# Hybrid decoder step on one core: order of the Mamba-2 scans, their decay rows and the state readouts in the mixer

## Chip, core and metric

The kernel runs on one core of a Trainium2 chip. A core has five engines that run beside each other, each through its own queue in order: TensorE (PE, matmuls and transposes; its weight loads are shown apart as PEld), VectorE (DVE), ScalarE (ACT), GpSimd (POOL) and SyncE (SP), which here only issues DMAs. The time is the device time of one execution in microseconds (us).

## What is computed

One step of a decoder trunk of depth 1 over 520 tokens: 512 of a new prompt and 8 samples that each carry on a sequence of their own. FFN1, a mixer and FFN2 follow each other, all float32. The mixer has two heads beside each other, and the change lies in the second one:

```python
proj = h @ w_in
u_pool, z, xbc, dt_raw = split(proj)
pool_out = pool_mix(u_pool)                       # causal means over 2, 4, 8, 16 tokens, then a matmul per group
xs, Bm, Cm = split(silu(causal_conv(xbc)))        # 1024 + 2*128 + 2*128 features
dt = softplus(dt_raw + dt_bias)
Acs = cumsum(dt * A)                              # within a chunk of 128 tokens, for each of 16 heads
y_diag = einsum(scores, exp(seg), dt, xc)         # inside the chunk
states = einsum(Bc, exp(Acs[-1] - Acs) * dt, xc)  # what the chunk adds to the state
...
y_off = einsum(Cc, h_prev, exp(Acs))              # what the state gives to the chunk
y = (y_diag + y_off + d_skip * xs) * silu(z)
y = rms_norm_per_group(y) * ssd_norm
out = concat([pool_out, y]) @ w_out
```

A sample has a chunk of one token, so its output is its old state, 128 numbers for each of 1024 features, times its C vector, scaled by its decay, plus the new token's own term. That product of state and C vector is called a readout below.

## The kernel before

Activations are kept feature by token: 128 features on the partitions, 520 tokens along them, worked in two halves of 260. A float32 matmul is made of three: high and low halves of weights and activations (`mm3`, L124, L127 and L128). An output tile of 128 features over 1024 inputs is 2 halves x 8 blocks x 3 = 48 matmuls. Its weights come by a DMA of SP, two tiles to a buffer ("raw", two buffers); ACT makes the high half (`whi`, L107), and the low half (`wlo`) is made either by DVE (L115) or, for tiles called late, by ACT (L111) and a DMA of POOL that adds the weights from memory (L112). There are three buffers for `whi` and `wlo`.

The mixer is cut into stages, each a letter and a number. Three strings of them (`CONV_PLAN`, `GATE_PLAN`, `LAST_PLAN`, L39 to L46) give the order in which the program is written; a scheduler then orders each engine's queue by simulated times, within pinned orders. The stages that the change concerns:

- `x0` to `x7`: a tile of the input projection, `inx`, followed by a convolution on DVE (U, A) and a Silu on ACT (L894), which makes a tile of X.
- `p`, `c`, `m`: a group of the pooling head. `p` is its projection `inp` and the running sums on POOL (PW, L924), `c` splits the result into high and low (`catp`, L938 and L939), `m` multiplies by the pooling weights (`pm` on PE).
- `A0` to `A7`: the first half of a scan step, `ssd_a`. A0 to A3 are the four chunks of head group 0, A4 to A7 those of group 1; names carry chunk and group, so `px01` is A4's. PE makes `pb` and transposes four tiles of X into `px`; SP loads the decay rows `ab` (L1071, 512 KB, three buffers) out of `scr_acs`; POOL and ACT make `we` (L1075, L1076), ACT the Exps `E` and `cd` and half of `ab`, DVE the other half (L1088); DVE makes `xdt` (L1093) from `px`, POOL `xw` (L1096), and DVE multiplies `ab` by the masked scores (L1097).
- `B0` to `B7`: the second half, `ssd_b`. PE multiplies `yo`, `pst` and `yd`; POOL and DVE bring the state `hst` on (L1118, L1119), DVE adds up `E` (L1122, L1123) and writes the output into X (L1126).
- `z0` to `z7`: a tile of the input projection for z, `inz`, with late weights; DVE moves its two halves out of PSUM (`zs`, L1136).
- `s2`: the next two samples of a group, `sample`. SP loads a C row (`cb`, L993, 64 KB) and a state (`h0`, L995, 256 KB, four buffers), and DVE makes four readouts of 128x128 (L998), pinned in program order. There are 16 sample and group pairs, so 64 readouts.
- `X`, `y`: small products of the samples (L988, L1004 and following). `G`, `H`: the gate, with a Silu over four z tiles at once, and its norm. `o`, `g`, `h`: thirds of the output projection `w_out`.

PE's outputs take one of eight PSUM banks each, in turn; a bank is free when its reader is done. SP, like every engine, issues in the order of its queue: a load that waits for its buffer holds those behind it.

Of the kernel before, what the change touches and what calls it, by code (L numbers as in the profile page):

```python
# [9 lines left out]
F32 = mybir.dt.float32  # L10
# [24 lines left out]
PAIRED = 3  # L35
ON_ACT = 4

CONV_PLAN = (
    "b0 b1 d0 b2 b3 x0 x1 v0 d1 x2 x3 d2 X0 p0 y0 c0 A0 p1 x4 m0 x5 B0 c1 p2 m1 A1 x6 c2 p3 A2 B1 x7 "  # L39
    "c3 X1 m2 A3 B2 e0"  # L40
)
# [20 lines left out]
def tile_trunk_step(ctx: ExitStack, tc: tile.TileContext, ins: dict, outs: dict):  # L62
# [30 lines left out]

    half, casts = [], []

# [6 lines left out]
    def split(src, n, name, hp, nb, tags, late=None):  # L102
# [7 lines left out]
        if late is not None:  # L110
            nc.scalar.activation(out=lo[:, q:], in_=src[:, q:], func=AF.Copy, scale=-1.0)  # L111
            nc.gpsimd.dma_start(out=lo[:, q:], in_=late, accum_op=ALU.add)  # L112
        if late is None or q:
# [649 lines left out]
def mixer(tc, ins, outs, e):  # L763
    nc = tc.nc
    cst, act, wp, tmp, dr, pool = (e[x] for x in ("cst", "act", "wp", "tmp", "dr", "pool"))
    ones = e["ones"]
    bank, load_unit, mm3, ws, v, rstd, rstds, vec, h, nx2, raw_tile, open_f2, fin, fill = (
        e[x] for x in ("bank", "load_unit", "mm3", "ws", "v", "rstd", "rstds", "vec", "h", "nx2", "raw_tile",
# [221 lines left out]

    def sample(b, g):
        cb = tmp.tile([P, HB], F32, tag="ta", name=f"cb{b}{g}")[:, :P]
        nc.sync.dma_start(out=cb, in_=rows_bc(b, 1, g))  # L993
        h0 = mp.tile([P, 4, P], F32, tag="h0", bufs=4, name=f"h0_{b}{g}")
        nc.sync.dma_start(out=h0, in_=ins["state_ssm"][:, b, 4 * g : 4 * g + 4])  # L995
        for q in range(4):
            tc.keep_in_program_order(
                nc.vector.scalar_tensor_tensor(out=junk, in0=h0[:, q], scalar=1.0, in1=cb, op0=ALU.mult, op1=ALU.mult,  # L998
                                               accum_out=ysm[:, 4 * g + q, b : b + 1]))

# [55 lines left out]
    pair = {}  # L1056

    def ssd_a(c, g):
        cs = slice(c * CH, (c + 1) * CH)
# [8 lines left out]
        for q in range(4):  # L1068
            nc.tensor.transpose(px[:, q * P : (q + 1) * P], X[:, 4 * g + q, cs], ident)
        ab = mp.tile([P, 8, P], F32, tag="ab", bufs=3, name=f"ab{c}{g}")  # L1070
        nc.sync.dma_start(out=ab, in_=scr_acs[c * NH + 8 * g : c * NH + 8 * g + 8].unsqueeze(0).to_broadcast([P, 8, P]))  # L1071
        dtc = tok[:, 0, c, 8 * g : 8 * g + 8]
# [108 lines left out]

    smp = [(b, g) for g in range(2) for b in range(NS)]

    def samples(n):
        for _ in range(n):
            if smp:
                sample(*smp.pop(0))

    pooled, box = [], {}

    def ssd(c):
        return c % NC, c // NC

    def outs_a():
# [15 lines left out]
        "s": samples,  # L1210
        "A": lambda j: ssd_a(*ssd(j)),
        "B": lambda j: ssd_b(*ssd(j)),
# [109 lines left out]
```

## Time and profile before

| what | value |
|---|---|
| runs | 971.78, 972.12 and 979.32 us, median 972.12 |
| profiled execution | 970.42 us, of which the span of its trace is 968.7 |
| granted TensorE clock | 0.997 of full |
| PE busy | 942.4 us, 97% |
| ACT, POOL busy | 694.3 us, 232.1 us |
| mixer | about 340 to 600 us of the span |

Busy time counts an engine's own instructions. In the chain of waits each step is followed back to what released it; the groups by line give busy time, the mean of one in ns, then the idle time of the engine ahead of it and who ended it. A row of the waits names the waiting engine and line, then who it waited for, and total, number of times and longest. In the timeline the columns are start, length, engine, line, operation, output and input. An answer for one line or tile gives shortest, median and longest duration, and for a DMA the same of the time from issue to landing.

### The profile page before, as it was taken

Reading aid. Unit: us, or ns where it says so; the run is one execution under the profiler, and the core shown is the slowest. Engines: PE = TensorE matmul, PEld = TensorE weight load, DVE = VectorE, ACT = ScalarE, POOL = GpSimd, SP = SyncE. Lnnn points to the kernel's source line nnn. Section 1 sums busy time; section 2 is a strip of 40 time slices with the busy share of each in tenths; the row PEclk is TensorE's granted clock in tenths of the full one; section 3 lists DMA queues with packets and bytes.
Section 4 is the critical chain, followed back from the end, with each engine's and each line's share of the span. In section 5 each row is a group of like instructions: output and inputs, shape, how many; then the busy total and the mean of one; then the engine's idle time right before and its main releaser. Section 6 shows DMA issues by size and latency. Waiting matters only on the chain.

```text
span 968.7 us, 20265 instructions
## 1 busy us (share of the span) xinstructions
PE 942.4 (97%) x7636; PEld 922.2 (95%) x7636; DVE 859.2 (89%) x1616; ACT 694.3 (72%) x1293; POOL 232.1 (24%) x341
## 2 busy tenths in 40 slices
PE   7999999999999999999999999999999999999995
PEld 6999999999999999989899999899999999999995
DVE  7999899989999698688989876999989999999986
ACT  8777677667767475686776556687788778887984
POOL 0111211121122000156523111122142223323430
PEclk9999999999999999999999999999999999999998
DMA  7565775675666243264598777466587668767852
GB/s 243 149 174 119 180 178 126 149 188 146 157 148 170 68 151 119 80 189 120 165 261 221 168 178 160 120 155 155 139 219 184 169 152 218 184 149 188 202 155 89
DMA packets 66739, 157.01 MB, mean 162 GB/s; under 512 B 9608, under 2 KB 22856, under 8 KB 66640
## 3 DMA queue, kind: packets, MB, share of 16 engines
q1 hardware_dynamic: 41168, 103.78, 34.0%
q0 software_dynamic: 25472, 51.92, 29.0%
q8 instruction: 60, 0.98, 0.4%
q14 instruction: 39, 0.32, 0.1%
HBM read 148.33 MB, written 7.34 MB: 161 GB/s over the span
## 4 chain that ended last, share of the span: by engine, by line
PE 86%; DVE 6%; DMA 3%; ACT 3%; issue 2%; POOL 0%; SPq 0%; DVEq 0%; ACTq 0%
PE A L128 8%; PE A L124 8%; PE A L127 8%; PE BE L128 6%; PE BE L124 6%; PE BE L127 6%; PE P L317 3%; PE wo L124 2%; PE wo L128 2%; PE wo L127 2%; PE A2d L127 2%; PE A2d L124 2%; PE A2d L128 2%; PE inz L124 2%; PE A1d L128 2%
## 5 line engine op out<-in xcount | busy, mean ns | idle before, releaser
L444 ACT COPY ac<-A 128x260 f32<-128x260 f32 x123 | 45.5, 370 | 17.0 <-PE A L128 16.6
L387 DVE TENSOR_TENSOR s<-raw 128x1024 f32<-128x1024 f32 x41 | 49.9, 1217 | 3.4 <-DMA raw<-in_w1gu 2.7
L124 PE MATMUL inz<-xh_mx,whi_inz 128*128 128x260 f32 x128 | 36.8, 287 | 1.0 <-DVE E L1122 1.0
L317 PE MATMUL P<-xg_f,raw 128*128 128x260 f32 x128 | 32.5, 407 | 5.3 <-DMA raw<-in_w1gu 5.3
L124 PE MATMUL wo<-catg,whi_wo 128*128 128x260 f32 x128 | 37.2, 290 | 0.0
L124 PE MATMUL inx<-xh_mx,whi_inx 128*128 128x260 f32 x128 | 36.4, 285 | 0.0
L128 PE MATMUL wo<-catg,wlo_wo 128*128 128x260 f32 x128 | 36.2, 283 | 0.0
L128 PE MATMUL inz<-xh_mx,wlo_inz 128*128 128x260 f32 x128 | 36.2, 283 | 0.0
L128 PE MATMUL inx<-xh_mx,wlo_inx 128*128 128x260 f32 x128 | 36.2, 283 | 0.0
L127 PE MATMUL inx<-xl_mx,whi_inx 128*128 128x260 f32 x128 | 36.1, 282 | 0.0
L127 PE MATMUL inz<-xl_mx,whi_inz 128*128 128x260 f32 x128 | 36.1, 282 | 0.0
L127 PE MATMUL wo<-catg,whi_wo 128*128 128x260 f32 x128 | 36.1, 282 | 0.0
L1028 POOL DMA_DIRECT2D out_nss<-hs x32 | 22.0, 688 | 52.1 <-DVE hs L1046 52.1
L317 PEld LDWEIGHTS P<-xg_f,raw 128*128 128x128 f32 x128 | 25.5, 204 | 9.2 <-ACT xg_f L193 5.2
L892 DVE SCALAR_TENSOR_TENSOR A<-U,h,A 128x544 f32<-128x544 f32 x36 | 28.1, 781 | 4.9 <-ACT A L890 4.6
L456 DVE TENSOR_TENSOR tg<-BE,ac 128x520 f32<-128x520 f32 x41 | 28.4, 693 | 2.8 <-PE BE L128 2.8
L466 DVE TENSOR_TENSOR tg<-tg,r_f 128x520 f32<-128x520 f32 x41 | 28.5, 695 | 2.7 <-ACT tg L464 2.6
L1146 DVE TENSOR_TENSOR h<-wo,h 128x260 f32<-128x260 f32 x48 | 19.4, 417 | 12.7 <-PE wo L128 12.7
L107 ACT CAST whi_wo<-raw_wo 128x1024 fp32r<-128x1024 f32 x12 | 12.6, 1046 | 24.7 <-issue 16.3
L998 DVE SCALAR_TENSOR_TENSOR junk<-h,cb 128x128 f32<-128x128 f32 x64 | 21.9, 343 | 9.1 <-DMA cb<-scr_bc 8.1
L464 ACT ACTIVATE tg<-tg 128x520 f32<-128x520 f32 x41 | 26.2, 639 | 3.9 <-DVE tg L463 3.9
L463 DVE TENSOR_TENSOR tg<-tg,r_f 128x520 f32<-128x520 f32 x41 | 28.4, 693 | 0.1
(1802 smaller groups left out, 4810.5 us busy)
## 6 DMA issues: line engine op xcount, KB each, us to landing
raw<-in_w2gu SPq DMA_DIRECT2D x44, 512.0 KB, 4.8
raw<-in_w1gu SPq DMA_DIRECT2D x42, 512.0 KB, 4.6
raw_1d<-in_w1d SPq DMA_DIRECT2D x24, 384.0 KB, 4.0
raw_2d<-in_w2d SPq DMA_DIRECT2D x24, 384.0 KB, 3.9
raw_wo<-in_w_out SPq DMA_DIRECT2D x12, 512.0 KB, 6.6
wlo_wo<-in_w_out POOLq DMA_DIRECT2D x12, 512.0 KB, 7.7
ab<-scr_acs SPq DMA_DIRECT2D x8, 512.0 KB, 5.7
h<-in_state_ssm SPq DMA_DIRECT2D x16, 256.0 KB, 7.4
```

The costliest lines, as they stand in the source:

```text
L124: first = nc.tensor.matmul(ps, whi, xhi, start=start, stop=False, **kw)
L127: nc.tensor.matmul(ps, whi, xlo, start=False, stop=False, **kw)
L128: nc.tensor.matmul(ps, wlo, xhi, start=False, stop=stop, **kw)
L317: nc.tensor.matmul(self.banks[f, u][b][:, :HB], ws(self.raw[f][:, u], j + 4 * q), xg[:, slot[q]], start=j == q == 0, stop=j == 3 and q == ...
L387: nc.vector.tensor_tensor(out=s1, in0=diag, in1=up0, op=ALU.add)
L444: nc.scalar.copy(keep, out[:, :HB])
L456: nc.vector.tensor_tensor(out=tg, in0=self.BE[k][:, :, :HB], in1=a, op=ALU.add)
L463: nc.vector.tensor_tensor(out=tg, in0=tg, in1=r, op=ALU.mult)
L464: nc.scalar.activation(out=tg, in_=tg, func=AF.Silu)
L466: nc.vector.tensor_tensor(out=tg, in0=tg, in1=r, op=ALU.mult)
L892: nc.vector.scalar_tensor_tensor(out=A[:, :n], in0=U[:, j : j + n], scalar=w(j), in1=A[:, :n], op0=ALU.mult, op1=ALU.add)
L1028: pin(nc.gpsimd.dma_start(out=js(outs["nss"], i), in_=t))
```

## The change

In the plans, x5 goes ahead of m0; A3 moves out of `CONV_PLAN` to behind z0, and A4 to behind z1; the samples begin at the end of `CONV_PLAN`, with two stages `s2`, and A7 comes behind the last `s2`. (What the line numbers of the changed kernel are called: +1 to +19 against those before; L1107 is L1088, L1112 is L1093, L1116 is L1097, L1003 is L998, L1145 is L1126, L1155 is L1136.)

```diff
 CONV_PLAN = (
-    "b0 b1 d0 b2 b3 x0 x1 v0 d1 x2 x3 d2 X0 p0 y0 c0 A0 p1 x4 m0 x5 B0 c1 p2 m1 A1 x6 c2 p3 A2 B1 x7 "
-    "c3 X1 m2 A3 B2 e0"
+    "b0 b1 d0 b2 b3 x0 x1 v0 d1 x2 x3 d2 X0 p0 y0 c0 A0 p1 x4 x5 m0 B0 c1 p2 m1 A1 x6 c2 p3 A2 B1 x7 "
+    "s2 c3 X1 s2 m2 B2 e0"
 )
 GATE_PLAN = (
-    "A4 z0 s2 B3 z1 s2 m3 z2 s2 B4 z3 s2 A5 z4 s2 B5 A6 z5 G0 s2 z6 A7 s2 z7 s2 B6 o0 H0 o1 B7 o2 G1 "
+    "z0 A3 z1 A4 B3 s2 m3 z2 s2 B4 z3 s2 A5 z4 s2 B5 A6 z5 G0 s2 z6 s2 A7 z7 B6 o0 H0 o1 B7 o2 G1 "
```

C rows are loaded two samples at a time (128 KB), one pair ahead, in two buffers of their own; a state's load is put behind the latest load of decay rows:

```diff
-    def sample(b, g):
-        cb = tmp.tile([P, HB], F32, tag="ta", name=f"cb{b}{g}")[:, :P]
-        nc.sync.dma_start(out=cb, in_=rows_bc(b, 1, g))
+    def sample_c(b, g):
+        cb = mp.tile([P, 2, P], F32, tag="cb", bufs=2, name=f"cb{b}{g}")
+        nc.sync.dma_start(out=cb, in_=scr_bc[b : b + 2, (2 + g) * P : (3 + g) * P].unsqueeze(0).to_broadcast([P, 2, P]))
+        return cb
+
+    def sample(b, g, cb):
         h0 = mp.tile([P, 4, P], F32, tag="h0", bufs=4, name=f"h0_{b}{g}")
-        nc.sync.dma_start(out=h0, in_=ins["state_ssm"][:, b, 4 * g : 4 * g + 4])
+        with tc.issue_after(held["ab"].ins):
+            held["h0"] = nc.sync.dma_start(out=h0, in_=ins["state_ssm"][:, b, 4 * g : 4 * g + 4])
...
+            reads.append(read.ins)
```

At the start of a scan its own decay rows and those of the next scan are loaded, unless they are already (`decay_rows`). The steps of scans 5, 6 and 7 are put, on each engine, behind the ninth-last readout (DVE), the last weight cast (ACT) and the last adding DMA (POOL) so far:

```diff
+    def decay_rows(j):
+        c, g = ssd(j)
+        ab = mp.tile([P, 8, P], F32, tag="ab", bufs=3, name=f"ab{c}{g}")
+        held["ab"] = nc.sync.dma_start(
+            out=ab, in_=scr_acs[c * NH + 8 * g : c * NH + 8 * g + 8].unsqueeze(0).to_broadcast([P, 8, P]))
+        return ab
...
+        k = g * NC + c
+        for j in (k, k + 1):
+            if j < 2 * NC and j not in rows:
+                rows[j] = decay_rows(j)
+        ab = rows[k]
...
+    def scan(j):
+        with ExitStack() as order:
+            if j >= FROM_LAST:
+                for ins_ in (reads[-9], casts[-1], adds[-1]):
+                    order.enter_context(tc.issue_after(ins_))
+            ssd_a(*ssd(j))
```

`adds` collects the adding DMAs of `split`. The first loads of `w_out` are put behind a state's load:

```diff
     def wout(cat, j, d2, fin=None):
-        wh, wl = load_unit(ins["w_out"][j, d2], 1024, f"wo{j}{d2}", True)
+        with tc.issue_after(held["wo"].ins) if j == 0 else nullcontext():
+            wh, wl = load_unit(ins["w_out"][j, d2], 1024, f"wo{j}{d2}", True)
...
+        if len(smp) == 2:
+            held["wo"] = held["h0"]
```

TensorE's queue at the end of x4, before: `inx41` is the second half of x4, `pm00` and `pm01` are the halves of m0, `inx50` the first half of x5.

```order
L127 MATMUL inx41_5516<-xl_mx_4325,whi_inx4_5511 128x260
L128 MATMUL inx41_5516<-xh_mx_4324,wlo_inx4_5512 128x260
L124 MATMUL pm00_5580<-catp_4689,wph_4690 128x260
L127 MATMUL pm00_5580<-catp_4689,wph_4690 128x260
L128 MATMUL pm00_5580<-catp_4689,wpo_4691 128x260
L124 MATMUL pm01_5586<-catp_4689,wph_4690 128x260
L127 MATMUL pm01_5586<-catp_4689,wph_4690 128x260
L128 MATMUL pm01_5586<-catp_4689,wpo_4691 128x260
L124 MATMUL inx50_5597<-xh_mx_4324,whi_inx5_5593 128x260
```

After, the same place in TensorE's queue, x4's end and x5's beginning:

```order
L125 MATMUL inx41_5518<-xh_mx_4324,whi_inx4_5513 128x260
L128 MATMUL inx41_5518<-xl_mx_4325,whi_inx4_5513 128x260
L129 MATMUL inx41_5518<-xh_mx_4324,wlo_inx4_5514 128x260
L125 MATMUL inx50_5587<-xh_mx_4324,whi_inx5_5583 128x260
L128 MATMUL inx50_5587<-xl_mx_4325,whi_inx5_5583 128x260
L129 MATMUL inx50_5587<-xh_mx_4324,wlo_inx5_5584 128x260
```

x5 now follows x4 at once. Further on in the same queue, at the end of x5 (`inx51` is its second half):

```order
L129 MATMUL inx51_5588<-xh_mx_4324,wlo_inx5_5584 128x260
L125 MATMUL inx51_5588<-xh_mx_4324,whi_inx5_5583 128x260
L128 MATMUL inx51_5588<-xl_mx_4325,whi_inx5_5583 128x260
L129 MATMUL inx51_5588<-xh_mx_4324,wlo_inx5_5584 128x260
L125 MATMUL pm00_5652<-catp_4689,wph_4690 128x260
L128 MATMUL pm00_5652<-catp_4689,wph_4690 128x260
L129 MATMUL pm00_5652<-catp_4689,wpo_4691 128x260
```

The 48 matmuls of x5 now stand ahead of m0's six.

TensorE's queue behind m2 (`pm21` is its second half), before: A3's `pb30` and `px30`, B2's `yo20`, `pst20` and `yd20`, A4's `pb01` and three quarters of `px01`, and the first matmul of z0 (`inz00`).

```order
L128 MATMUL pm21_6099<-catp_4689,wpo_4691 128x260
L1061 MATMUL pb30_6105<-ident_4617,BC_4632 128x128
L1062 MATMUL pb30_6105<-BC_4632 128x128
L1069 MATMUL px30_6112<-ident_4617,X_4631 128x128 x4
L1106 MATMUL yo20_6142<-BC_4632,hst_4699 128x128 x4
L1109 MATMUL pst20_6147<-xw20_5989,bt20_5958 128x512
L1112 MATMUL yd20_6149<-ab20_5967,xdt20_5987 64x128 x8
L1061 MATMUL pb01_6174<-ident_4617,BC_4632 128x128
L1062 MATMUL pb01_6174<-BC_4632 128x128
L1069 MATMUL px01_6181<-ident_4617,X_4631 128x128 x3
L124 MATMUL inz00_6214<-xh_mx_4324,whi_inz0_6209 128x260
```

Three scan steps stand there directly behind each other. After, the same place in TensorE's queue:

```order
L129 MATMUL pm21_6131<-catp_4689,wpo_4691 128x260
L1125 MATMUL yo20_6137<-BC_4632,hst_4699 128x128 x4
L1128 MATMUL pst20_6142<-xw20_5991,bt20_5960 128x512
L1131 MATMUL yd20_6144<-ab20_5782,xdt20_5989 64x128 x8
L125 MATMUL inz00_6177<-xh_mx_4324,whi_inz0_6172 128x260
```

Only B2 is left ahead of z0. Then, in the same queue, the end of z0 (`inz01` is its second half):

```order
L129 MATMUL inz01_6178<-xh_mx_4324,wlo_inz0_6173 128x260
L1077 MATMUL pb30_6229<-ident_4617,BC_4632 128x128
L1078 MATMUL pb30_6229<-BC_4632 128x128
L1085 MATMUL px30_6236<-ident_4617,X_4631 128x128 x4
L125 MATMUL inz10_6272<-xh_mx_4324,whi_inz1_6267 128x260
```

A3 stands between z0 and z1. Then the end of z1 (`inz11`):

```order
L129 MATMUL inz11_6273<-xh_mx_4324,wlo_inz1_6268 128x260
L1077 MATMUL pb01_6324<-ident_4617,BC_4632 128x128
L1078 MATMUL pb01_6324<-BC_4632 128x128
L1085 MATMUL px01_6331<-ident_4617,X_4631 128x128 x4
L1125 MATMUL yo30_6356<-BC_4632,hst_4699 128x128 x4
L1128 MATMUL pst30_6361<-xw30_6263,bt30_6232 128x512
L1131 MATMUL yd30_6363<-ab30_5969,xdt30_6261 64x128 x8
L125 MATMUL pm30_6394<-catp_4689,wph_4690 128x260
```

z0's 48 matmuls now stand ahead of A3's and z1's ahead of A4's, and the four quarters of `px01` are together. From z2 on TensorE's order is as before. On VectorE, 16 readouts stand ahead of the output of B3 (before: one).

VectorE's queue around scan 5 (names with 11), before: its L1088 stands ahead of B3's `E30`, and no readout is ahead of that.

```order
L1097 TENSOR_TENSOR ab01_6186<-ab01_6186,scm01_6179 128x1024
L1088 TENSOR_SCALAR ab11_6569<-ab11_6569,tok_4686 128x128 x2
L892 SCALAR_TENSOR_TENSOR A7_6072<-U7_6071,h_69,A7_6072 128x544
L1088 TENSOR_SCALAR ab11_6569<-ab11_6569,tok_4686 128x128 x2
L1122 TENSOR_TENSOR E30_6122<-yo30_6282,E30_6122 128x512
```

Its subtractions are early. Further on in the same queue, before, its `xdt11` and L1097 among readouts of the seventh and eighth state of group 0:

```order
L1093 TENSOR_TENSOR xdt11_6589<-px11_6564,tok_4686 128x512
L998 SCALAR_TENSOR_TENSOR junk_4697,ysm_4695<-h0_60_6543,cb60_6541 128x128 x2
L1066 TENSOR_TENSOR scm11_6562<-pb11_6557,tri_4619 128x128
L998 SCALAR_TENSOR_TENSOR junk_4697,ysm_4695<-h0_70_6551,cb70_6549 128x128
L1097 TENSOR_TENSOR ab11_6569<-ab11_6569,scm11_6562 128x1024
```

They stand among the readouts, with nothing of group 1 ahead. After, VectorE's queue behind the last readout of group 0 (`h0_01` and `h0_11` are the first two states of group 1, `cb01` their pair of C rows):

```order
L1107 TENSOR_SCALAR ab11_6336<-ab11_6336,tok_4686 128x128 x4
L1012 TENSOR_TENSOR ysm_4695<-ysm_4695,sdec_4693 128x32
L1013 TENSOR_TENSOR ysm_4695<-ysm_4695,xb0_6796 128x32
L1180 SCALAR_TENSOR_TENSOR X_4631<-X_4631,h_69,ysm_4695 128x8 x4
L1011 TENSOR_TENSOR xb1_7252<-sxdt_4694,sbc_4696 128x32
L1155 TENSOR_TENSOR zs_6169<-inz31_6502,r_mx_4327 128x260
L1003 SCALAR_TENSOR_TENSOR junk_4697,ysm_4695<-h0_01_6555,cb01_6465 128x128 x2
L1112 TENSOR_TENSOR xdt11_6599<-px11_6574,tok_4686 128x512
L1003 SCALAR_TENSOR_TENSOR junk_4697,ysm_4695<-h0_01_6555,cb01_6465 128x128 x2
L1082 TENSOR_TENSOR scm11_6572<-pb11_6567,tri_4619 128x128
L1003 SCALAR_TENSOR_TENSOR junk_4697,ysm_4695<-h0_11_6561,cb01_6465 128x128
L1116 TENSOR_TENSOR ab11_6336<-ab11_6336,scm11_6572 128x1024
```

Scan 5's L1107 (L1088 before) now stands behind all 32 readouts of group 0, and its `xdt11` and L1116 behind two and five readouts of group 1.

More of the change, by code (lines that the diff above doesn't have):

```diff
@@ L111, in split @@
             nc.scalar.activation(out=lo[:, q:], in_=src[:, q:], func=AF.Copy, scale=-1.0)
-            nc.gpsimd.dma_start(out=lo[:, q:], in_=late, accum_op=ALU.add)
+            adds.append(nc.gpsimd.dma_start(out=lo[:, q:], in_=late, accum_op=ALU.add).ins)
         if late is None or q:
@@ L1056, in mixer @@
     pair = {}
+    rows, reads = {}, []
+    def decay_rows(j):
[4 more added lines that the diff above has]
+        return ab
     def ssd_a(c, g):
@@ L1180, in gate_out @@
                                            op0=ALU.mult, op1=ALU.subtract)
-    smp = [(b, g) for g in range(2) for b in range(NS)]
+    smp = [(b, g) for g in range(2) for b in range(0, NS, 2)]
+    cbs = []
     def samples(n):
-        for _ in range(n):
-            if smp:
-                sample(*smp.pop(0))
+        (b, g), ahead = smp.pop(0), smp[:1]
+        if not cbs:
+            cbs.append(sample_c(b, g))
+        cbs.extend(sample_c(*x) for x in ahead)
+        cb = cbs.pop(0)
+        for q in range(n):
+            sample(b + q, g, cb[:, q])
+        if len(smp) == 2:
+            held["wo"] = held["h0"]
     pooled, box = [], {}
@@ L1210, in mixer @@
         "s": samples,
-        "A": lambda j: ssd_a(*ssd(j)),
+        "A": scan,
         "B": lambda j: ssd_b(*ssd(j)),
```

12 lines of the change are left out of this document (6 added, 6 removed).

## The prediction

> **What bounds the kernel now.** I read the busy shares and the chain first, then stretches of the span, then the waits of TensorE.
>
> ```profile
> PE 942.4 (97%) x7636; PEld 922.2 (95%) x7636; DVE 859.2 (89%) x1616; ACT 694.3 (72%) x1293; POOL 232.1 (24%) x341
> PE 86%; DVE 6%; DMA 3%; ACT 3%; issue 2%; POOL 0%; SPq 0%; DVEq 0%; ACTq 0%
> ```
>
> TensorE (PE) is busy for 942.4 of 968.7 us and is 86% of the chain that ended last. No change that leaves its matmuls alone can win more than its 26.3 us of idle time. The question is how much of that lies where the change works.
>
> ```profile
> 340.00:430.00 90.00, 88.67 (x733) 87.00 (x733) 72.92 (x158) 60.40 (x116) 16.19 (x49) 1.00 0.43 139
> 430.00:472.00 42.00, 39.96 (x338) 36.74 (x336) 36.74 (x72) 28.05 (x50) 28.01 (x46) 1.00 0.46 134
> 472.00:510.00 38.00, 37.95 (x318) 35.32 (x320) 33.46 (x126) 30.63 (x54) 11.13 (x14) 1.00 0.81 220
> 510.00:560.00 50.00, 50.00 (x423) 47.85 (x420) 44.71 (x140) 27.56 (x39) 11.44 (x12) 1.00 0.77 198
> 625.00:969.00 344.00, 328.62 (x2696) 325.08 (x2694) 316.79 (x542) 267.67 (x556) 98.18 (x140) 0.99 0.67 168
> ```
>
> Columns: the stretch, its length, busy us of PE, PEld, DVE, ACT and POOL, the granted clock, the DMA share, GB/s. The change touches roughly 425 to 560 us. There PE idles 1.33 us before 430, 2.04 up to 472, 0.05 up to 510 and nothing after. The 15.4 us of idle behind 625 lie in the second FFN, which the change does not edit; I carry them unchanged. Who ends the waits in the mixer:
>
> ```profile
> PE pm L127 <- DVE catp L939: 1.3, 1, 1.3
> PE px L1069 <- DVE xdt L1093: 1.1, 1, 1.1
> PE inz L124 <- DVE E L1122: 1.0, 1, 1.0
> ```
>
> Three waits, one time each, all ended by VectorE (DVE): 1.3 + 1.1 + 1.0 = 3.4 us. The chain of waits shows what stood ahead:
>
> ```profile
> 425.76 1.19 DVE ab L1097
> 426.95 0.71 DVE catp L939 x2
> 427.70 0.39 PE pm L127
> ...
> 468.17 1.71 DVE ab L1088 x4
> ...
> 471.40 0.61 DVE E L1122
> 472.06 0.39 PE inz L124
> ```
>
> At 427.70 the pooling product m0 waited for its low part (L939), queued on DVE behind a scan's decay product (L1097). At 469 to 472 DVE had the steps of scans 2, 3 and 4 at once, and PE had nothing else in its queue.
>
> **The change part by part.** First, x5 goes ahead of m0. Its 48 matmuls, at 37.95 us for 318, take 5.7 us. PE, free for them at 426.4 (427.70 less the wait), comes to m0 at about 432.1, four us after L939 ended. The cover needs x5's weights early enough:
>
> ```profile
> 419.78 1.22 DVE L115 TENSOR_TENSOR wlo_inx<-raw_inx,whi_inx 128x1024 fp32r<-128x1024 f32 x1
> ```
>
> They stand at 421.0, five us before PE could start x5. Worth **-1.33**, and if the cover were gone just that comes back.
>
> Second, scan 3's first half moves behind z0 and scan 4's behind z1. PE then runs pm, B2, z0, A3, z1, A4, B3. Between the steps that asked for DVE together there are now 48 matmuls each time, against waits of 1.1 and 1.0 us. Worth **-2.1**. PE then reaches z0 about 3.4 us plus the two moved first halves earlier; nothing in the trace idles between there and 560, so the gain survives only if what PE needs comes as much earlier. Three supplies may not.
>
> (a) **Silu of x7.** It makes the last columns of X: the fourth transpose of A4 reads them on PE, and on DVE the small product with the sample columns (L990 after) stands ahead of the evacuation of z0, whose PSUM bank I expect B3's first product to take. ScalarE (ACT) has scan 5's Exp in front of it, which waits for decay rows that SyncE (SP) issues directly behind out_ncp.
>
> ```profile
> 469.56 0.34 SPq L1195 DMA_DIRECT2D out_ncp<-ncp  x1
> 482.47 1.28 ACT L894 ACT_TABLE_LOAD   x1
> 483.76 0.63 ACT L894 ACTIVATE X<-A 128x512 f32<-128x512 f32 x1
> ...
> 478.06 0.89 PE yo L1106 x8
> ...
> 480.84 0.32 PE inz L124
> ...
> 484.64 0.13 PE px L1069
> L107 ACT CAST whi_inz<-raw_inz 128x1024 fp32r<-128x1024 f32 x8 | 8.3, 1042 | 10.3 <-PE inz L127 5.4 <-PE inx L127 4.0 <-PE inp L127 0.9
> L1081 ACT ACTIVATE E<-ab 64x512 f32<-64x512 f32 x12 | 7.5, 628 | 10.6 <-DVE X L1126 9.9 <-DMA ab<-scr_acs 0.4
> ```
>
> For the landing of such rows, from the answers for the decay line (L1071) and then for the C line (L993):
>
> ```profile
> DMA to landing us min/median/max: 3.3/5.7/8.0
> ...
> DMA to landing us min/median/max: 2.9/5.4/10.0
> ```
>
> With the 1.33 us gained before it, out_ncp goes at 468.2 and scan 5's rows at 468.6; they land at 474.3 by the median, 476.6 by the longest. Then come two Exps (0.63 each), one copy of a weight half (about 1.04, as the cast), two small pieces (my estimate 0.4), the table load 1.28 and Silu 0.63: 4.6 us, so 478.9 or 481.2; product and evacuation add my estimate of 0.6. PE wants it at 484.64 less 3.4, less B3's 2.8 us (478.06 to 480.84, now behind), plus what z1 had left (5.7 less 3.8, now ahead): about 480.4. So 0 to 1.4 us are lost, and 0.4 more if PE is earlier than I count. I take **+0.6**, between ends 0 and 1.8.
>
> (b) **Scan 5 behind the readouts.** Its four DVE subtractions stood ahead of every readout; now they follow all 32 of group 0, and its xdt follows two readouts of group 1, which wait for a C pair of their own.
>
> ```profile
> L998 DVE SCALAR_TENSOR_TENSOR junk<-h,cb x64: 275/291/1080, 485.3 to 541.5; 128x128 f32<-128x128 f32 x64
> ...
> L1093 DVE TENSOR_TENSOR xdt<-px,tok 128x512 f32<-128x512 f32 x8 | 5.5, 681 | 0.0
> L1097 DVE TENSOR_TENSOR ab<-ab,scm 128x1024 f32<-128x1024 f32 x8 | 10.4, 1303 | 0.1
> ...
> 493.28 0.12 PE inz L128
> ...
> 509.51 1.02 PE yd L1112 x16
> ```
>
> The pair's buffer is free when the 24th readout is done, which stands behind z2's second evacuation. z2 ended at 493.28, now 489.9; with 0.4 for the evacuation and two readouts, 491.1. Landed at 496.5 by the median, 501.1 by the longest C row. Five readouts at 0.29 and an accumulator read of about 0.08 each (1.9), xdt 0.68, the mask product (estimate 0.3) and L1097 1.30 make 4.2: 500.7 or 505.3. B5's yd wants it at 509.51 - 3.4 = 506.1. Hidden by 0.8 even at the longest; but a pair is twice the bytes and other DVE work stands between. Ends 0 and 1.5, **+0.3**, nearer to the hidden side.
>
> (c) **z7's weights.** POOL's accumulate-DMA finishes them.
>
> ```profile
> L112 POOL DMA_DIRECT2D wlo_inz<-in_w_in x8: 866/872/887, 451.9 to 511.2; - x8
> DMA to landing us min/median/max: 5.3/8.2/9.2
> ...
> 523.73 0.12 PE inz L124
> ```
>
> The last goes at 511.2 and lands by 520.4 at the longest, 3.3 us ahead of z7. If it stays where it was while PE comes 3.4 earlier, 0.1 is missing. Its cast now follows the gate's Silu without a table load between, but scans 5 and 6 leave Exps and a POOL product in front. Ends 0 and 1.5, **+0.3**.
>
> At nothing: eight C loads for sixteen (SP is not on the chain), decay rows one scan ahead (their waits fell on POOL and ACT, not PE), w_out's first load behind the twelfth state load (its first matmul comes behind B6, after all that is named here), and fewer, larger DMA issues. A gain from any of these has no idle PE time to show in.
>
> The sum: -3.4 + 0.6 + 0.3 + 0.3 = **-2.2 us**. The profiled execution takes 970.42 (span 968.7 and 1.7 around it), so 968.2. The shown median of 972.12 lies 1.7 above that execution; against it the forecast is **969.9 us**.
>
> **The rivals.** *All of it is gained*: (a) to (c) stay hidden. 972.1 - 3.4 = 968.7. For it: each is hidden at its median landing. Against: three at once, on a DMA share of 0.81 from 472 to 510.
>
> *Readouts meet POOL.* Readouts move from after 485 into a stretch where POOL works more (28.0 of 42 us before 472, 11.1 of 38 after).
>
> ```profile
> 462.27 2.92 POOL L924 TENSOR_TENSOR PW<-PW 128x652 f32<-128x652 f32 x2
> ...
> 461.36 4.25 DVE X L1126 x4
> ...
> L1126 DVE SCALAR_TENSOR_TENSOR X<-X,h,E x24: 332/343/2214, 461.4 to 556.8; 128x128 f32<-128x128 f32 x24
> ```
>
> Four instructions with a median of 0.34 us took 4.25 together while POOL ran two pooling sums: 2.9 us more. Readouts too reach 1.08 us against 0.29. If B3's POOL products hold the readouts that now stand around z0's and z1's evacuations as long, and PE waits for those banks, 2.9 of 3.4 us are given back: -0.5, 971.6. Against: the pooling sums end ahead of z0, and DVE has slack once scans 3 and 4 are apart. The Trainium skill, "SBUF — State Buffer", section "Who interferes with whom", says that a VectorE instruction with two SBUF inputs contends with a GpSimd instruction that reads SBUF, and that the one which started first blocks the other for its whole length. By that rule every readout moved is exposed; the long row agrees with it, and the median of 343 ns leaves open how often it bites.
>
> *Slower: scan 5's decay rows land late.* Place: SP at 468, (a)'s chain. Break-even is when Silu of x7 ends 3.4 us after PE wants it, that is a landing about 11 us behind the issue. The state loads show that such times occur (answer for L995):
>
> ```profile
> DMA to landing us min/median/max: 3.2/7.4/11.6
> ```
>
> At 13 us (the DMA share rises as state loads move forward), Silu ends at 486.2, B3 at 486.8 and not 480.4: +6.4 - 3.4 = +3.0, 975.1. Against: the eight decay loads took at most 8.0.
>
> *The change does not do what it says*, since queue order differs and waits simply reappear unnamed: 972.1.
>
> **How the numbers follow.** Forecast 0.52; all gained 0.13; POOL 0.15; slower 0.14; nothing 0.06. The first, second and third make 0.80 with points from 968.7 to 971.6; with the upper ends of (a) to (c) lost, 4.8 in all, the time is 973.5, and the quickest and middle run shown differ by 0.3. The range is 968.0 to 974.3, which cuts the slower case in its lower part. A measurement of this kernel can tell about 1% (9.7 us) from no change: no case reaches 962.4, since idle PE time in reach is 3.4; only several delays together reach 981.8. Faster 0.02, within 0.94, slower 0.04.
>
> **What would show it.** In the changed profile the three wait rows are gone from PE between 335 and 625, and z0 starts near 467. (a) shows as a PE wait on px or yo near 480, ended by ACT's Silu or by the evacuation of z0; (b) as one on yd near 506; (c) as one ended by DMA on inz near 520. Mixer idle of about 1.2 us bears me out; 3 or more refutes the sum. Readouts of 1 us and longer between 465 and 485 speak for POOL; scan 5's rows landing 11 us or more behind their issue for the slower case.

## The result and the profile after

| | before | changed |
|---|---|---|
| median of 15 runs each | 975.67 us (969.72 to 980.74) | 967.85 us (966.66 to 969.38) |
| profiled execution | 970.42 us, span 968.7 | 967.68 us, span 965.8 |
| ratio | 1 | 0.9935, 95% interval 0.9917 to 0.9953 |

Two numbers stand there, and they are not the same. The two profiled executions differ by 2.7 us, the forecast 2.2 and a little of drift ahead of the mixer. The medians differ by 7.8 us, since the runs of before are spread over 11 us and those of the changed kernel over 2.7. The profile of before that the prediction was made from was one of its short runs. The forecast was 969.9 us, in a range from 968.0 to 974.3; the measured 967.85 lies 2.0 below the forecast and just below the range.

The page of the changed kernel, busy time and chain, has TensorE (PE) at the same 97%:

```profile
PE 941.3 (97%) x7636; PEld 921.6 (95%) x7636; DVE 860.6 (89%) x1616; ACT 694.5 (72%) x1293; POOL 231.4 (24%) x341
PE 75%; DVE 11%; ACT 5%; issue 3%; DMA 3%; POOL 1%; SPq 1%; DVEq 0%; ACTq 0%; POOLq 0%
```

The stretches of the changed kernel (columns as before: length, busy us of PE, PEld, DVE, ACT and POOL, clock, DMA share, GB/s):

```profile
340.00:430.00 90.00, 90.00 (x747) 88.69 (x747) 73.06 (x157) 61.18 (x118) 17.49 (x49) 1.00 0.37 127
430.00:472.00 42.00, 42.00 (x357) 39.21 (x356) 37.37 (x75) 28.89 (x52) 28.14 (x47) 1.00 0.60 175
472.00:510.00 38.00, 37.06 (x316) 34.20 (x316) 35.96 (x146) 24.62 (x45) 10.50 (x12) 1.00 0.83 221
510.00:560.00 50.00, 49.23 (x410) 47.05 (x409) 46.16 (x123) 34.56 (x46) 10.95 (x12) 1.00 0.77 193
```

PE's idle time of 1.33 and 2.04 us ahead of 472 is gone; 0.94 and 0.77 us have come behind it. The waits of PE in the changed kernel, 335 to 625 us, name them:

```profile
PE A L125 <- ACT ac L445: 0.9, 2, 0.5
PE yd L1131 <- DVE zs L1155: 0.9, 1, 0.9
PE inz L129 <- DMA wlo_inz<-in_w_in: 0.8, 1, 0.8
```

So 3.4 us were won and 1.7 given back in the mixer. The first matmul of w_out shows the net; from the chains of waits of before and of the changed kernel:

```profile
532.25 0.32 PE wo L124
```

```profile
529.61 0.33 PE wo L125
```

2.6 us earlier, of which some 0.3 stood there already ahead of the mixer (the first matmul of its norm, `psr_mx`, starts at 358.1 and at 357.8). 2.3 us is the mixer's own share. The waits alone net 1.7; the other 0.6 us stands in no row of the waits, but in stretches in which PE counts as busy, and no run here splits it.

### The profile page after: what moved, and what is told of

It reads as the page before. It is cut to its first block, busy times and chain, and to the rows that moved or that the text cites. A ratio compares the mean times of both kernels' runs of the same rounds, so it can differ in the third digit from the quotient of the medians.

```text
span 965.8 us, 20249 instructions
## 1 busy us (share of the span) xinstructions
PE 941.3 (97%) x7636; PEld 921.6 (95%) x7636; DVE 860.6 (89%) x1616; ACT 694.5 (72%) x1293; POOL 231.4 (24%) x341
## 4 chain that ended last, share of the span: by engine, by line
PE 75%; DVE 11%; ACT 5%; issue 3%; DMA 3%; POOL 1%; SPq 1%; DVEq 0%; ACTq 0%; POOLq 0%
PE A L129 8%; PE A L125 8%; PE A L128 8%; PE BE L129 6%; PE BE L128 5%; PE BE L125 5%; PE wo L125 2%; PE wo L129 2%; PE wo L128 2%; PE A2d L128 2%; PE A2d L125 2%; PE A2d L129 2%; PE A1d L129 2%; PE A1d L128 2%; PE A1d L125 2%
## 5 line engine op out<-in xcount | busy, mean ns | idle before, releaser
L389 DVE TENSOR_TENSOR s<-s,raw 128x512 f32<-128x512 f32 x41 | 28.0, 682 | 0.0
```

The costliest lines, as they stand in the source:

```text
L389: nc.vector.tensor_tensor(out=s2[:, 0], in0=s1[:, 1], in1=raw[:, 0, :nb], op=ALU.add)
```

## The experiments

| kernel | runs | median | lowest, highest | before on the same chip |
|---|---|---|---|---|
| before_again | 12 | 973.86 | 969.92, 977.79 | 975.08 |
| x5_first | 12 | 972.19 | 969.55, 978.24 | 975.08 |
| scans_apart | 12 | 974.99 | 972.64, 977.17 | 975.08 |
| hold_off | 12 | 975.64 | 973.64, 978.12 | 975.08 |
| before_hold | 12 | 971.67 | 969.69, 977.24 | 974.30 |
| c_single | 12 | 969.69 | 968.49, 971.88 | 974.30 |
| no_pool30 | 7 | 967.35 | 966.07, 970.15 | 974.30 |
| better | 12 | 968.87 | 966.49, 972.26 | 974.30 |
| late_readouts | 12 | 973.49 | 970.84, 977.28 | 972.91 |
| x1_later | 12 | 968.71 | 967.55, 974.02 | 972.91 |
| late_x1 | 12 | 974.42 | 971.23, 977.01 | 972.91 |
| before_third | 8 | 975.82 | 972.01, 980.44 | 974.55 |

The first question was where the spread of before comes from and which part of the change ends it.

### before_again: no edit

> The kernel before, unchanged, for its spread: its 15 runs lie at 969.7 to 972.7 us (7) and at 975.7 to 980.7 us (8), while the 15 of the changed kernel lie at 966.7 to 969.4. Theory A (the change saves the three PE waits, 3.4 us, and pays 1.7 us of new ones, and the slower half of the runs of before has nothing to do with the mixer): the times fall in the same two groups, and a profile of 975 us or more, if one is caught, shows its extra time outside 420 to 560 us. Theory B (in before a step of the mixer is late in half of the runs, and the change also takes that away): such a profile shows 5 us or more of extra PE wait between 420 and 560 us.

Its runs lie evenly from 969.9 to 977.8, not in two groups. The profile fell on a run of 971.3 us and showed the three known waits alone in the part that the change touches, so it told the theories apart no further. Its record has a granted clock of 0.95 from one end of the mixer to the other, yet its matmuls come as fast as at 1.00 (45 from 485 to 490 us, against 44 in the first profile of before); that one record of the clock is therefore not taken as a slower clock.

### x5_first: one part alone

```diff
-    "... p1 x4 m0 x5 B0 c1 ..."
+    "... p1 x4 x5 m0 B0 c1 ..."
```

> Before with x5 ahead of m0 alone. Both theories: the PE wait for catp L939 (1.3 us) is gone, the waits of 1.1 and 1.0 us at scan 4 and z0 stay, profile 1.3 us shorter than before's fast runs, 969.1. If the wait for catp comes back under another name: 970.4. Theory A: the two groups of times stay. Theory B: they may go.

The wait for catp is gone and no wait took its place at m0. The ratio to before is 0.9967 (0.9945 to 0.9990), 3 us in the median; the interval runs from 1.0 to 5.4 us and so holds the 1.3 us of the wait. The spread stayed, and this time the profile fell on the longest run, 978.24 us. Its waits of PE:

```profile
PE psr_y L171 <- DVE E L1122: 3.5, 1, 3.5
PE px L1069 <- DVE xdt L1093: 1.2, 1, 1.2
PE inz L124 <- DVE E L1122: 1.0, 1, 1.0
PE px L1069 <- ACT X L894: 0.7, 1, 0.7
```

And its stretches (the clock is the third number from the end):

```profile
472.00:477.00 5.00, 5.00 (x31) 5.00 (x31) 4.68 (x12) 2.58 (x8) 0.30 (x1) 0.67 0.98 193
477.00:482.00 5.00, 5.00 (x45) 4.07 (x44) 4.09 (x9) 3.08 (x7) 2.99 (x2) 1.00 0.05 11
537.00:542.00 5.00, 2.89 (x23) 2.48 (x21) 0.00 (x0) 3.09 (x4) 0.33 (x1) 1.00 0.99 230
542.00:547.00 5.00, 3.57 (x14) 3.16 (x15) 4.53 (x21) 1.63 (x3) 0.54 (x1) 0.66 0.95 239
```

Read the third column's count: 31 matmuls in five busy microseconds instead of 44 or 45. PE counts as busy all along, but its granted clock is 0.67. The two waits of 1.2 and 1.0 us, which every profile of before has too (0.8 to 1.2 us), were here followed by a slow stretch that cost another 13 matmuls of 0.12 us, 1.6 us; the wait of 3.5 us near 541 was followed by one too. In the first profile of before the same pair of waits was followed by a clock of 1.00 throughout. So a wait of PE has two prices: itself, and in some runs the clock behind it. The second is in no row of the waits.

The 3.5 us can be followed one step further. VectorE (DVE) stood still for a C row that SyncE issued at 534.18, and the `E` that PE waited for stood behind that readout:

```profile
542.47 0.29 DVE L998 SCALAR_TENSOR_TENSOR junk<-h,cb 128x128 f32<-128x128 f32 x1 [6.76 <-DMA cb<-scr_bc]
```

So in a kernel that has before's readouts, loads and scans, a late C row can cost PE 3.5 us and the clock.

### scans_apart: the other move alone

```diff
-    "c3 X1 m2 A3 B2 e0"
+    "c3 X1 m2 B2 e0"
...
-    "A4 z0 s2 B3 z1 s2 m3 z2 ..."
+    "z0 A3 z1 A4 s2 B3 s2 m3 z2 ..."
```

> Before with A3 behind z0 and A4 behind z1, the readouts in stages as late as they were, C rows one by one, no hold on scans 5 to 7. Theory A: the PE waits at scan 4 and z0 (2.1 us) are gone, the wait for catp L939 (1.3) stays; new waits under 0.9 since no readouts stand ahead of z0's evacuation: profile 968.3 to 969.2. Rival (a queue full of scan steps behind z0 moves the wait into yd of B3): 970 and more. Theory B: this part or x5_first ends the slower group of runs.

The two waits near 470 went, as expected, and the time did not: 974.99, ratio 0.9993 (0.9975 to 1.0011). This profile has waits of PE near 540 instead, for the norm of the output (`psr_y`) and for w_out's bank (1.7 and 1.9 us), again with a clock under 0.9 behind them. By itself this move, the 2.1 of my 3.4 us, shows no gain, though the interval's lower end would just hold 2.1 us.

### hold_off: the hold on scans 5 to 7 taken away

```diff
-FROM_LAST = 5
+FROM_LAST = 8
```

> The changed kernel with the hold on scans 5 to 7 off (FROM_LAST = 8); PE's order is the same. Theory A, that z7's weights are late since the gate's Silu waits behind scan 6's last Exp on ACT, which waits for scan 6's four subtractions held behind the readouts on DVE: the Silu starts about 3 us earlier, the wait inz <- DMA wlo_inz of 0.8 us goes, the wait of yd (0.9) stays, 966.9 against 967.7. Rival (the DMA itself was slow): the wait stays within 0.3 of 0.8. Theory B on the spread: if the hold is what steadies the times, a slower group 5 us or more above comes back here.

All 12 runs lie between 973.6 and 978.1: the whole gain is gone (ratio to before 1.0012, 0.9995 to 1.0029), the case that theory B left open. Theory A was right on the small point: the gate's Silu starts at 504.69 and no z weight is waited for, though PE also comes to z7 some 10 us later here. It missed on yd of B3, which does not wait for z0's evacuation in this run: L990 took 0.18 us. What it costs shows in the waits of PE:

```profile
PE pst L1128 <- POOL xw L1115: 4.8, 1, 4.8
...
PE yd L1131 <- DVE ab L1116: 1.3, 1, 1.3
```

The 4.8 us can be followed back through three queues of the same profile (SyncE, VectorE, SyncE, VectorE):

```profile
486.95 0.38 SPq L1070 DMA_DIRECT2D ab<-scr_acs  x1
...
495.88 0.29 DVE L1107 TENSOR_SCALAR ab<-ab,tok 128x128 f32<-128x128 f32 x1 [4.01 <-ACT E L1100]
...
500.33 0.38 SPq L995 DMA_DIRECT2D cb<-scr_bc  x1
...
507.69 0.29 DVE L1003 SCALAR_TENSOR_TENSOR junk<-h,cb 128x128 f32<-128x128 f32 x1 [3.02 <-DMA cb<-scr_bc]
```

Scan 6's decay rows are issued at 486.95. Without the hold scan 6's subtraction stands on VectorE among the readouts of the fourth and fifth states, and DVE stands still for 4.0 us until those rows have landed and ScalarE (ACT) has read them. The readouts behind it end later, the C pair's buffer is free later, the first C pair of group 1 is issued at 500.33 and not waited out until 507.69, and scan 5's xdt and POOL's xw stand behind it. PE's clock:

```profile
507.00:512.00 5.00, 2.07 (x2) 0.50 (x2) 4.28 (x12) 1.14 (x2) 3.09 (x4) 0.63 1.08 386
512.00:517.00 5.00, 3.77 (x25) 3.44 (x26) 5.00 (x16) 2.63 (x4) 0.00 (x0) 0.50 0.65 154
517.00:522.00 5.00, 5.00 (x38) 5.00 (x38) 5.00 (x13) 1.82 (x5) 1.62 (x2) 0.85 0.70 186
```

This is my prediction's mechanism (b), with the sign turned: I took the hold, which puts scan 5's steps behind the readouts, for a risk. It is the other way about. A step that waits for a DMA blocks the readouts in front of which it stands, and the readouts free the buffers that the next loads need. (FROM_LAST takes the hold away on VectorE, ScalarE and POOL together; no run takes it away on one engine alone.)

### before_hold: the hold alone, added to before

```diff
...
+                for ins_ in (reads[-9], casts[-1], adds[-1]):
+                    order.enter_context(tc.issue_after(ins_))
...
```

> Before with the hold on scans 5 to 7 alone added; PE's order is before's. Theory H (in the kernel without the hold, scan 5's or 6's subtractions stand on DVE ahead of readouts and wait there for their decay rows, the readouts and the C loads behind them come late, PE then waits 3 us or more once, and its granted clock falls for some 5 us after that): the hold alone steadies before, all runs within 969 to 973, median 971.5, no stretch of 5 us with a clock under 0.9 between 500 and 560. Rival S (before's slow runs come from its sixteen single C loads, issued late on SP): the median stays at 975 with runs up to 979.

971.67, ratio 0.9985 (0.9960 to 1.0010); the interval holds both no gain and the 2.6 us by which the medians differ. Six of twelve runs are under 972, but four lie from 973.1 to 977.2: the hold alone does not steady before. The profile, of a run of 970.43 us, has the three old waits and a clock of 1.00. Theory H holds in part only; something else lengthens runs of before.

### c_single: C rows one by one

```diff
...
-        cbs.extend(sample_c(*x) for x in ahead)
-        cb = cbs.pop(0)
         for q in range(n):
-            sample(b + q, g, cb[:, q])
+            cb = tmp.tile([P, HB], F32, tag="ta", name=f"cb{b + q}{g}")[:, :P]
+            nc.sync.dma_start(out=cb, in_=rows_bc(b + q, 1, g))
+            sample(b + q, g, cb)
```

> The changed kernel with C rows loaded one sample at a time, each when its sample comes, as before; PE's order is the same. Theory H: within 1.5 us of the changed kernel, 967 to 970, since the hold keeps the readouts moving. Rival S: the wait DVE junk <- DMA cb grows from 0.7 us to 5 or more, PE waits 3 us once between 500 and 545 and the clock falls after it: 973 and more, in half of the runs at least.

969.69, highest 971.88, on a chip where before has 974.30: ratio 0.9945 (0.9925 to 0.9965). Rival S is out for the changed kernel: with the hold and the early readouts in place, sixteen single C loads do not bring the spread back. That they do no harm in before's own order is not shown; the long run of x5_first waited for one of them. What pairs may be worth, some 1 to 2 us between kernels timed on different chips, stays unsettled.

### late_readouts: the readouts as late as before

```diff
-    "s2 c3 X1 s2 m2 B2 e0"
+    "c3 X1 m2 B2 e0"
...
-    "z0 A3 z1 A4 B3 s2 m3 z2 s2 B4 z3 s2 A5 z4 s2 B5 A6 z5 G0 s2 z6 s2 A7 z7 B6 ..."
+    "z0 A3 z1 A4 s2 B3 s2 m3 z2 s2 B4 z3 s2 A5 z4 s2 B5 A6 z5 G0 s2 z6 A7 s2 z7 s2 B6 ..."
```

> The changed kernel with the readouts in stages as late as before (first ones behind A4); PE's order is the same. What the early readouts are worth. Theory Q: they are what made yd of B3 late (with POOL) and they hold scan 6's decay rows behind four more state loads on SP; without them the yd wait is 0.2 or less, those rows are issued before 480 and not at 484.8, no z weight waits over 0.3, profile 966.2, median 966.5 to 968 on a chip where the changed kernel has 968. Rival R: the readouts then crowd in behind 485 as in before, DVE waits 5 us and more for C rows, and PE waits 1 us or more between 500 and 560 or the clock falls there: 970 and more in half of the runs.

Rival R: 973.49, ratio 0.9999 (0.9973 to 1.0024). The early readouts, which I had listed as a danger to z0's evacuation, are as necessary as the hold. The waits of PE and one stretch of this profile (974.59 us):

```profile
PE yd L1131 <- DVE ab L1116: 2.2, 1, 2.2
PE psr_y L172 <- DVE E L1141: 1.6, 1, 1.6
PE pst L1128 <- POOL xw L1115: 1.0, 1, 1.0
```

```profile
510.00:515.00 5.00, 5.00 (x33) 4.67 (x29) 4.97 (x27) 3.66 (x3) 0.09 (x1) 0.55 0.91 184
```

Scan 5's steps are held behind readouts that now come late (its xdt stands behind one that waited 3.7 us for a C row), so the hold without early readouts makes B5 late, which is just what (b) said.

### late_x1: the same, with X1 later

```diff
-    "c3 X1 m2 B2 e0"
+    "c3 m2 B2 e0"
...
-    "z0 A3 z1 A4 s2 B3 s2 m3 ..."
+    "z0 A3 z1 A4 s2 B3 X1 s2 m3 ..."
```

> The kernel late_readouts with X1 behind B3 too. Theory Q: within 0.4 of late_readouts, since without early readouts nothing holds z0's evacuation; the best of all, 966 to 967. Rival R: as for late_readouts.

974.42, with the same waits of yd (2.2) and psr_y (1.9). It bears late_readouts out.

### before_third: no edit, for a longer run

> The kernel before once more, unchanged, for a profile of one of its longer runs (about half of its runs lie above 974). If the profile is above 974: theory H has it lose its extra time between 465 and 560 us, as a PE wait of over 1.5 us for a scan's product or an evacuation behind readouts that wait for C rows, followed by a granted clock under 0.9 for some 5 us; the rival has the extra time in one of the FFNs, with the mixer as in the first profile. If it is below 973, it tells nothing and the mixer shows the three known waits alone.

The profile fell on 973.39 us, the second shortest of the eight runs and between the two cases of the expectation. Its extra wait of PE in the mixer:

```profile
PE px L1069 <- ACT X L894: 2.3, 1, 2.3
```

It lies where theory H put it, but no readout that waits for a C row makes it. Behind it the clock falls (the stretch 485 to 490 has 23 matmuls):

```profile
485.00:490.00 5.00, 4.24 (x23) 4.24 (x24) 4.10 (x17) 4.91 (x10) 0.79 (x1) 0.68 0.98 262
```

PE waited for Silu of x7, which ACT ran at 485.08. What made it late is on POOL and DVE; rows of their timelines in this profile:

```profile
476.79 2.36 POOL L1075 TENSOR_TENSOR we<-ab,tok 128x8 f32<-128x8 f32 x1 [4.40 <-DVE scm L1066]
...
476.58 0.77 DVE L892 SCALAR_TENSOR_TENSOR A<-U,h,A 128x544 f32<-128x544 f32 x1
477.27 0.68 DVE L939 TENSOR_TENSOR catp<-PW,catp 128x512 fp32r<-128x512 f32 x1
477.87 1.21 DVE L1097 TENSOR_TENSOR ab<-ab,scm 128x1024 f32<-128x1024 f32 x1
...
485.08 0.63 ACT L894 ACTIVATE X<-A 128x512 f32<-128x512 f32 x1
```

The same instruction in the first profile of before, and what DVE did then:

```profile
477.63 0.21 POOL L1075 TENSOR_TENSOR we<-ab,tok 128x8 f32<-128x8 f32 x1 [4.04 <-DMA ab<-scr_acs]
...
477.57 0.28 DVE L1066 TENSOR_TENSOR scm<-pb,tri 128x128 f32<-128x128 f32 x1
```

A POOL product of eight numbers a partition took 2.36 us and not 0.21. It began just behind a DVE instruction with two inputs in SBUF, and ended with the third of them in a row. In the first profile it fell into the moment in which DVE read `pb` out of PSUM. ACT's Exp of `we`, scan 5's E and, in order, the Silu stood behind it. A few tenths of a microsecond decide whether 2 us go, and then the clock is lost as well. This is read from the times of the rows; no run moved that product alone.

### no_pool30: the POOL products of scan 3 left out

```diff
-        nc.gpsimd.tensor_tensor(out=xw, in0=xdt, ...)
+        if (c, g) == (3, 0):
+            xw = xdt
...
+            if (c, g) != (3, 0):
                 nc.gpsimd.tensor_tensor(out=hv8, in0=hv8, ...)
```

> The changed kernel without two products of POOL in scan 3: the state is not scaled by its decay (L1137) and pst takes xdt instead of xw (L1115), so the states from chunk 3 of group 0 are others; PE's order is the same. Theory L (a readout of 1.02 us and the sample product L990 of 1.03 us, alone 0.29 and 0.19, were held by these two POOL products, and that made yd of B3 0.9 us late): both are short, DVE reaches z0's evacuation 1.5 us earlier, the yd wait is 0 to 0.1, profile 966.8 against 967.7. Rival (the eight readouts ahead of the evacuation by themselves make it late, or x7's Silu does): L990 stays long or waits, yd waits 0.7 to 0.9.

In the changed kernel's timeline two DVE instructions are long, each beside a POOL product:

```profile
476.71 1.02 DVE L1003 SCALAR_TENSOR_TENSOR junk<-h,cb 128x128 f32<-128x128 f32 x1
480.54 1.03 DVE L990 TENSOR_TENSOR sxdt<-sdt,X 128x32 f32<-128x32 f32 x1
481.50 0.41 DVE L1155 TENSOR_TENSOR zs<-inz,r_mx 128x260 f32<-128x260 f32 x1
...
476.55 1.04 POOL L1115 TENSOR_TENSOR xw<-xdt,we 128x512 f32<-128x512 f32 x1 [6.09 <-DVE xdt L1112]
480.25 1.28 POOL L1137 TENSOR_TENSOR hst<-hst,cd 128x512 f32<-128x512 f32 x1 [1.47 <-PE yo L1125]
...
481.96 1.09 PE L1131 MATMUL yd<-ab,xdt 128*64 128x128 f32 x16 [0.94 <-DVE zs L1155]
```

Without the two products, the answer for L990 is

```profile
L990 DVE TENSOR_TENSOR sxdt<-sdt,X x2: 184/226/267, 417.9 to 480.3; 128x32 f32<-128x32 f32 x2
```

and yd no longer waits; PE waits 0.4 for Silu of x7 instead and 0.3 for z7. The kernel gives 967.35 us, profile 967.35 against 967.68; one profile each, 0.3 us apart, does not show what the 0.9 us is worth at the end. Theory L is shown for the wait: POOL's products made yd wait, and (a)'s Silu, hidden behind it till then, is the next thing late.

### better, x1_later: two tries to win the 1.7 us back

```diff
-    "s2 c3 X1 s2 m2 B2 e0"
+    "s2 c3 s2 m2 B2 e0"
...
-    "z0 A3 z1 A4 B3 s2 m3 z2 s2 B4 z3 s2 A5 z4 s2 B5 A6 z5 G0 s2 ..."
+    "z0 A3 z1 A4 B3 X1 s2 m3 z2 s2 B4 z3 s2 A5 z4 s2 B5 G0 A6 z5 s2 ..."
```

(x1_later has the move of X1 alone.)

> The changed kernel with the sample product X1 behind B3 in the plan and the gate G0 ahead of A6; PE's order is the same. My theory of the two new waits: z0's evacuation no longer stands behind L990, so yd's wait of 0.9 us falls to 0.1 or less, and the gate's Silu no longer waits for scan 6's Exp, so z7's weights come 3 us earlier and the wait of 0.8 is gone: 966.0 against 967.7, 1.7 less. Rival (one more ACT table load and the gate's products ahead of scan 6's subtractions make scan 6 late): z7's wait gone, but a wait of 1 us or more at px21, pst21 or yd21 near 525, no gain or a loss.

> The changed kernel with X1 alone put behind B3 in the plan; all orders but DVE's are the same. Theory Q: yd's wait falls from 0.9 to 0.2 as it did with the gate moved too, the wait for z weights stays between 0.8 and 2.3, since it hangs on the landing of scan 6's decay rows: 967.0. Rival: PE comes 0.7 earlier to weights that come no earlier, the wait for them grows by 0.7, no gain, 967.7.

Both took yd's wait away (0.2 and none), and both lost it again at the weights. The waits of PE in better, then in x1_later:

```profile
PE inz L129 <- DMA wlo_inz<-in_w_in: 2.3, 1, 2.3
```

```profile
PE inz L129 <- DMA wlo_inz<-in_w_in: 2.0, 2, 1.4
```

The long one is at z5 (it ends at 511.15 and at 508.08), not at z7. Its cast stands on ACT behind a step of scan 6 that waits for decay rows, in the changed kernel and in better:

```profile
492.26 0.22 ACT L1102 ACTIVATE cd<-ab 128x8 f32<-128x8 f32 x1 [7.19 <-DMA ab<-scr_acs]
```

```profile
494.75 0.22 ACT L1102 ACTIVATE cd<-ab 128x8 f32<-128x8 f32 x1 [8.08 <-DMA ab<-scr_acs]
```

Those rows are issued by SyncE behind state loads that wait for a buffer. PE that comes earlier meets weights that come no earlier. For the gate's earlier place my theory was right where it was made (z7 no longer waits), the rival right on the sum; for x1_later the rival was right, the wait for weights grew. Neither kernel beats the changed one: their ratios to before on the same chip are 0.9930 and 0.9942, against 0.9935. A fourth buffer for the decay rows might free them from the state loads; it was not run.

## Why the prediction came out as it did

- **The three waits removed, 3.4 us:** gone in the changed kernel, as in its parts x5_first and scans_apart. Right, and by the mechanism named.
- **(a), 0.6 of 0 to 1.8:** measured 0.9, at yd of B3, by the evacuation of z0 as written, but Silu of x7 was not the cause. It ended at 478.8, as the working had it (478.9), and DVE did not wait for it. DVE was late itself, behind eight readouts, one of which and L990 stood beside POOL products, which is the mechanism of the POOL rival at a third of its price. The step that failed is the assumption that the one supply I could time was the one that would end last.
- **(b), 0.3 of 0 to 1.5:** nothing. L1116 of scan 5 ended at 504.25 and yd wanted it at 505.77. The margin of 1.5 us lies inside the bounds worked out, but the sign of the hold was read wrongly: hold_off shows that without it the same scan costs 4.8 us of waiting and the clock.
- **(c), 0.3 of 0 to 1.5:** measured 0.8, at z7. The DMA went at 513.01 and took 8.02 us. The gate's Silu ran at 508.88 instead of 504.63, since scan 6's last Exp stands ahead of it and that waits for subtractions held behind readouts. In hold_off, with the Silu back at 504.69, there is no such wait, but PE also comes later to z7 there; the chain is read from the changed kernel's own rows.
- **The sum:** -2.2 against a mixer that gained 2.3 and profiles that differ by 2.7. That they lie so close is in part luck. With (a) to (c) as measured the sum is -3.4 + 0.9 + 0 + 0.8 = -1.7, and a gain of 0.6 us that the sum does not have, and that no wait names, makes up for the rest.
- **The median:** the step that failed is "the shown median of 972.12 lies 1.7 above that execution; against it the forecast is 969.9". It took the runs shown (971.78, 972.12, 979.32) as one time with noise. Over 15 runs before has 975.67. Two sentences of the working failed with it: that no change can win more than the 26.3 us of idle time, and that a gain from the loads put at nothing "has no idle PE time to show in"; the early readouts and the hold stand in the sum as risks alone. PE that counts as busy can run at half its clock, as in x5_first, and the idle time of one short execution leaves out the waits of the long ones. The spread has causes in the mixer that can be seen: a POOL product that takes ten times as long (before_third), readouts and C rows late for group 1 (x5_first shows it with before's readouts, hold_off and late_readouts in kernels without one of the parts), and behind each the clock. The record of the runs agrees: of the 124 other runs of before (the odd record of before_again left out), the 9 with a mean granted clock of 0.997 took 969.18 to 975.16 us, the 16 with 0.991 or less 977.79 to 982.53. All 15 of the changed kernel have 0.996 or 0.997. The change narrows the spread from 11.0 to 2.7 us, and that, not the 2.3 us, is most of the 7.8.
- **Which part does it:** no one part gives the whole. The hold alone gives 0.9985, the moves of the scans alone 0.9993, x5 alone 0.9967; the whole without the hold 1.0012, without the early readouts 0.9999. Readouts that start early and scans that wait behind them need each other: early readouts free the state and C buffers in time, and the hold keeps a step that waits for a DMA from standing in front of them. That neither works alone is measured; that this is the reason is read from the traces of hold_off and late_readouts.
- **Open:** the share of each cause in the long runs of before. None of its runs above 974 us has a profile: two profiles of before and one of before_hold fell on short runs, the third of before on 973.39. Open too is what the parts of the hold on the single engines, the places of the state loads and the later first loads of `w_out` are worth apart.

The slower rival, scan 5's rows landing 11 us or more behind their issue, did not come: the eight loads of the changed kernel took at most 8.0 us.

## What to carry to other kernels

In a kernel whose TensorE is busy for 97%, ask of each wait not only how long it is but whether it can grow: PE met x7's Silu without a wait in one execution of before and waited 2.3 us for it in another. Such a wait costs its length and can cost the clock behind it, and the median shows what one profile hides. Put a step that waits for a DMA behind the work that frees buffers on its engine, not in front of it, and start that work early enough that the order costs nothing. Where several runs are given, look at their spread before the sum is made.

## What the runs showed of the hardware

The granted clock of TensorE fell to 0.50 for stretches of 3.41 us: one behind 2.3 us of waiting (before_third), one behind 1.2 and 1.0 us close together and one behind 3.5 us (x5_first), three in a row behind 4.8 us (hold_off), two behind late_readouts' waits of B5. It stayed at 1.00 behind 1.1 and 1.0 us in the first profile of before and behind 2.3 us in better. The traces show what tells these cases apart. Within a trace all such stretches begin on one grid of 3.41 us: in x5_first the one at 543.58 comes 21 lengths behind the one at 471.90. In a window of that grid x5_first had both its waits, 1.83 us of idle time; in the first profile of before they fell into two windows, with 1.24 and 0.85 us. The windows of x5_first, then of before:

```profile
468.49:471.90 3.41, 1.58 (x11) 1.34 (x12) 3.41 (x9) 3.41 (x10) 3.41 (x6) 1.00 0.28 59
471.90:475.31 3.41, 3.41 (x18) 3.41 (x17) 3.09 (x9) 2.67 (x7) 0.40 (x1) 0.50 0.95 173
```

```profile
467.79:471.20 3.41, 2.17 (x23) 1.53 (x22) 3.41 (x8) 3.41 (x7) 3.41 (x7) 1.00 0.05 9
471.20:474.61 3.41, 2.56 (x21) 2.56 (x22) 3.00 (x9) 3.41 (x12) 2.31 (x4) 1.00 0.27 102
```

Laid through all fourteen profiles from 10 to 950 us, the grid has eight windows at full clock with 1.74 us or more of idle time, and each is followed by a fall; no other window at full clock has more than 1.56 us, and none is followed by one. The 2.3 us in better were split into 0.89 and 1.39. So what counts here is how much of one window is idle, about half being enough, and the same wait costs the clock or not by where the window's edge falls in that run. The Trainium skill, "TensorE: Matmul & The Clock Gate", section "Part 1: The HAM clock gate (the "warmup" mystery)", has the clock halve after an idle window of about 3.4 us, in windows that run freely. The half clock, the length and the free windows agree with the traces; that the window must be idle does not, since 1.74 of 3.41 us were enough.

POOL and VectorE held each other up in both directions: a readout of 0.29 us took 1.02 and a product of 0.19 to 0.27 took 1.03 beside POOL products, and a POOL product of 0.21 took 2.36 beside three VectorE instructions with two SBUF inputs in a row. The rule cited in the prediction from "SBUF — State Buffer" of the Trainium skill, that the one which starts first blocks the other for its whole length, agrees with the first kind, where POOL's product began first. In the second the POOL product ended just behind the third VectorE instruction, not behind the first.
